# Batched matrix product: output copied out of PSUM in blocks of 32 partitions instead of 64, and one batch's blocks on VectorE

## The chip, the cores and the metric

The kernel runs on one core of a Trainium2 chip. The metric is the device time of one execution in microseconds (us). Before the change it is 136.78 us, the median of three runs (136.75 to 137.25).

The core's engines work side by side and wait for each other through semaphores: TensorE (PE in the profile; PEld is its weight load), VectorE (DVE), ScalarE (ACT), GpSimd (POOL) and SyncE (SP), which here only issues DMAs. Matrix products land in PSUM. VectorE and ScalarE copy them from there into SBUF, and DMAs carry them on to HBM. Each engine runs its instructions in the order in which they stand in the program.

## The reference

```python
batch, dim_i, dim_j, dim_k = 32, 256, 512, 384
# x: (batch, dim_i, dim_j) float32, y: (batch, dim_j, dim_k) float32

def reference(x, y):
    return np.einsum('bij,bjk->bik', x, y).astype(np.float32)
```

For each of 32 batches a 256x512 matrix is multiplied by a 512x384 matrix. The sum runs over j.

## The kernel before

**Stages.** The 32 batches are taken in N = 8 groups of Q = 4. Stage n handles batches 4n to 4n+3. Within a stage each batch has 32 partitions of its own in x, y and the weights: batch g has partitions 32g to 32g+31.

**Loads (lines 64 to 77).** `x_sb` has 128 partitions with 8 rows of 512 floats each (2 MB in all; each partition reads 16 KB in one run). `y_sb` has 128 partitions with 16 rows of 384 floats each (3 MB; 24 KB in one run). In the last stage y comes in four parts. SP issues all DMAs. There are two buffers each for x and y, so the load for stage n+2 waits until VectorE has cast stage n's data.

**x (lines 79 to 96), on VectorE.** x is cast to fp16 (`x_r`, line 83). Two neighbouring fp16 values are then taken as one 32-bit word and transposed in blocks of 32x32 words into `xt_sb`. `width(n)` chooses between two layouts. The 256 rows of a batch are spread over its 32 partitions, 8 rows each. Row r of a partition goes into half e (r modulo 2 in both layouts), and within the half it gets a column of the weights. With NARROW (64) the eight rows split as (b h e) with two values for each, and a transpose handles one e and one b: four transposes of 128x512 words a stage (line 96), with destination words two apart. With WIDE (32) they split as (h e) with four values of h, and a transpose handles one e: two transposes of 128x1024 words (line 90), with destination words next to each other. In both, source words are TW = 8 words apart. So the width sets which of a batch's 256 output rows lies in which partition of the result.

**y and the matmuls (lines 98 to 120).** y is cast to fp16 in four pieces on VectorE (line 107). After each piece come the matmuls for it: for both halves e, for the four t of the piece, for the four batches g, a matmul that contracts 32 partitions and adds into `ps_of[n][e][g]`, a PSUM tile of 128x384 floats. The four batches sit in four row tiles of the array. There are 128 matmuls a stage. The eight result tiles take all eight buffers of the PSUM pool (`bufs=2 * Q`), so a stage's matmuls into a tile wait until the stage before has been copied out of the same tile.

**Copying out (`collect`, lines 122 to 140).** With w = 64, `per` is 2: each of the eight result tiles is copied in two blocks of 64x384 into `o_sb`, 16 copies a stage. Two batches share the 128 partitions of an output part, 64 partitions each. All copies run on ScalarE, except in the last stage, where g = 1 and g = 3 go to VectorE.

**Stores (`store`, lines 142 to 153).** A partition of `o_sb` holds Q/`per` runs of output. With w = 64 those are two runs of 4 rows (6 KB), and each stage has two stores of 768 KB.

**Order (lines 155 to 166).** Every instruction is pinned to program order with `keep`. Two loads come first. Then for each n: cast and transpose x, cast y with the matmuls, copy out, load n+2, and store stage n−1. The last three stores (DEFER = 3) follow the loop. VectorE's order before is thus, for each stage: x cast, four transposes, four y casts; only in the last stage eight copies follow. SP's order is: x load n+2, y load n+2, stores of n−1.

Of the kernel before, what the change touches and what calls it, by code (L numbers as in the profile page):

```python
# [1 line left out]

# [5 lines left out]


MM_DT = mybir.dt.float16  # L10
F32 = mybir.dt.float32
P = 128


Q = 4
WIDE = 32
NARROW = 64

DEFER = 3


@with_exitstack
def kernel(
    ctx: ExitStack,
    tc: tile.TileContext,
    x: bass.AP,
    y: bass.AP,
    out: bass.AP,
):
    nc = tc.nc  # L30

    B, I, J = x.shape
    _, _, K = y.shape

    PQ = P // Q
    R = I // PQ
    T = J // PQ
    TW = T // 2
    NE = I // P
    N = B // Q  # L40

    x_pool = ctx.enter_context(tc.tile_pool(name="x_pool", bufs=2))
    y_pool = ctx.enter_context(tc.tile_pool(name="y_pool", bufs=2))
    xr_pool = ctx.enter_context(tc.tile_pool(name="xr_pool", bufs=1))
    xt_pool = ctx.enter_context(tc.tile_pool(name="xt_pool", bufs=2))
    yr_pool = ctx.enter_context(tc.tile_pool(name="yr_pool", bufs=2))
    o_pool = ctx.enter_context(tc.tile_pool(name="o_pool", bufs=DEFER + 2))
    psum_pool = ctx.enter_context(
        tc.tile_pool(name="psum", bufs=2 * Q, space=bass.MemoryType.PSUM)
    )  # L50

    keep = tc.keep_in_program_order

    x_of, y_of, xt_of, yr_of, ps_of, o_of = {}, {}, {}, {}, {}, {}

    def width(n):
        return NARROW

    def pieces(n):
        return 4

    def load(n):
        x_of[n] = x_pool.tile([P, R, J], F32, name="x_sb")
        keep(
            nc.sync.dma_start(  # L67
                out=x_of[n],
                in_=x[n * Q : (n + 1) * Q].rearrange("g (p r) j -> (g p) r j", r=R),
            )  # L70
        )
        y_of[n] = y_pool.tile([P, T, K], F32, name="y_sb")
        src = y[n * Q : (n + 1) * Q].rearrange("g (q t) k -> (g q) t k", t=T)
        parts = 4 if n == N - 1 else 1
        for a in range(parts):
            s = slice(a * T // parts, (a + 1) * T // parts)
            keep(nc.sync.dma_start(out=y_of[n][:, s], in_=src[:, s]))  # L77

    def transpose_x(n):


        x_r = xr_pool.tile([P, R, J], MM_DT, name="x_r")
        keep(nc.vector.tensor_copy(x_r, x_of.pop(n)))  # L83
        xt_of[n] = xt_pool.tile([P, NE, TW, P], F32, name="xt_sb")
        words = x_r.bitcast(F32)
        if width(n) == WIDE:
            src = words.rearrange("p (h e) (q t) -> p e t h q", e=NE, t=TW)
            dst = xt_of[n].rearrange("p e t (h s) -> p e t h s", s=PQ)
            for e in range(NE):
                keep(nc.vector.transpose(dst[:, e], src[:, e]))  # L90
        else:
            src = words.rearrange("p (b h e) (q t) -> p b e t h q", b=2, e=NE, t=TW)
            dst = xt_of[n].rearrange("p e t (h s b) -> p b e t h s", s=PQ, b=2)
            for e in range(NE):
                for b in range(2):
                    keep(nc.vector.transpose(dst[:, b, e], src[:, b, e]))  # L96

    def multiply(n):
        xt = xt_of.pop(n).bitcast(MM_DT).rearrange("p e t (m c) -> p e t m c", c=2)
        y_sb = y_of.pop(n)  # L100
        y_r = yr_pool.tile([P, T, K], MM_DT, name="y_r")
        ps_of[n] = [
            [psum_pool.tile([P, K], F32, name="o_ps") for _ in range(Q)] for _ in range(NE)
        ]
        step = T // pieces(n)
        for a in range(0, T, step):
            keep(nc.vector.tensor_copy(y_r[:, a : a + step], y_sb[:, a : a + step]))  # L107
            for e in range(NE):
                for t in range(a, a + step):
                    for g in range(Q):  # L110
                        s = slice(g * PQ, (g + 1) * PQ)
                        keep(
                            nc.tensor.matmul(  # L113
                                ps_of[n][e][g],
                                xt[s, e, t // 2, :, t % 2],
                                y_r[s, t],
                                start=(t == 0),
                                stop=(t == T - 1),
                            )
                        )  # L120

    def collect(n):
        w = width(n)
        per = P // w
        o_of[n] = o_pool.tile([P, R, K], F32, name="o_sb")
        o = o_of[n].rearrange("p (u f) k -> p u f k", u=Q // per)
        for u in range(Q // per):
            for e in range(NE):
                for v in range(per):
                    g = u * per + v  # L130
                    ps = ps_of[n][e][g]
                    on_vector = n == N - 1 and g % 2 == 1
                    for h in range(per):
                        src = ps[h * w : (h + 1) * w]
                        dst = o[v * w : (v + 1) * w, u, h * NE + e]
                        if on_vector:
                            keep(nc.vector.tensor_copy(dst, src))  # L137
                        else:
                            keep(nc.scalar.copy(dst, src))  # L139
        del ps_of[n]  # L140

    def store(n):
        w = width(n)
        per = P // w
        o = o_of.pop(n).rearrange("p (u f) k -> p u f k", u=Q // per)
        for u in range(Q // per):
            b = n * Q + u * per
            keep(
                nc.sync.dma_start(
                    out=out[b : b + per].rearrange("g (s f) k -> (g s) f k", s=w),  # L150
                    in_=o[:, u],
                )
            )

    for n in range(2):
        load(n)
    for n in range(N):
        transpose_x(n)
        multiply(n)
        collect(n)  # L160
        if n + 2 < N:
            load(n + 2)
        if n + 2 - DEFER >= 0 and n + 2 < N:
            store(n + 2 - DEFER)
    for n in range(N - DEFER, N):
        store(n)


# [1 line left out]
_INS = ['x', 'y']  # L170
_OUTS = [((32, 256, 384), 'float32')]


# [23 lines left out]
```

## Time and profile before

| What | Value |
|---|---|
| Median of three runs | 136.78 us |
| The profiled execution's own time | 137.25 us |
| Its span, first to last instruction | 135.5 us |
| TensorE (matmul) busy | 64.2 us, 47% |
| VectorE busy | 83.6 us, 62% |
| ScalarE busy | 58.0 us, 43% |
| Mean DMA rate over the span | 404 GB/s of 54.68 MB |
| Mean granted TensorE clock | 0.783 |

Some groups of instructions, as the page lists them:

| Line, engine | Instruction | Count | Mean ns |
|---|---|---|---|
| 83, VectorE | cast of x, 128x4096 | 8 | 2294 |
| 96, VectorE | transpose, 128x512 words | 32 | 1072 |
| 107, VectorE | cast of a piece of y, 128x1536 | 32 | 953 |
| 139, ScalarE | copy out of PSUM, 64x384 | 120 | 473 |
| 137, VectorE | copy out of PSUM, 64x384 | 8 | 556 |

How to read it: the span runs from the first to the last instruction of one execution. The chain of waits follows the work that ended last back to the start, at each step to what released it. A line of the timeline gives the start in us, the duration in us, the engine, the line of the code, the operation with output and input, its count, and in brackets how long the engine had been idle before and what released it. DMA rows cut the span into 40 equal slices, with a digit for the busy tenths of each.

The time at which each stage's x cast starts (line 83) is, in us: 8.80, 21.05, 34.26, 46.48, 63.46, 79.29, 95.63 and 111.82.

### The profile page before, as it was taken

The numbers are of one execution on the slowest core, as the hardware profiler recorded it, in microseconds if no ns is written. First come the engines' busy times: TensorE is split into PE (matmuls) and PEld (weight loads), VectorE is DVE, ScalarE is ACT, GpSimd is POOL, SyncE is SP. The second block draws the span as 40 slices with busy tenths as digits, with TensorE's granted clock in tenths as the row PEclk, the third lists the DMA queues.
The fourth block names the chain that finished last, engine by engine and source line by source line (L and its number), as shares of the span: only waits on it lengthen the run. The fifth ranks groups of instructions, "written<-read, shape, count | busy, mean of one in ns | idle before, by whom it ended". The sixth has DMA issues, their size and how long they took to land.

```text
span 135.5 us, 2381 instructions
## 1 busy us (share of the span) xinstructions
PE 64.2 (47%) x1024; PEld 33.7 (25%) x1024; DVE 83.6 (62%) x80; ACT 58.0 (43%) x121; POOL 0.2 (0%) x4
## 2 busy tenths in 40 slices
PE   0000099309934793579408940099302970089500
PEld 0000056104612361136104520045101540045200
DVE  0049777947897596822979059670796509990660
ACT  3000000894089408940794079500795039800640
POOL 0000000000000000000000000000000000000000
PEclk9999999975797579757975698556985698556985
DMA  4999999999999998999999999999999999999765
GB/s 111 426 431 457 414 445 450 389 428 474 392 435 421 435 399 339 442 441 450 398 399 453 423 457 385 415 431 457 418 385 417 441 409 419 415 421 426 302 279 210
DMA packets 5050, 54.68 MB, mean 404 GB/s; under 512 B 560, under 2 KB 560, under 8 KB 3120
## 3 DMA queue, kind: packets, MB, share of 16 engines
q1 hardware_dynamic: 5040, 54.53, 96.2%
q8 instruction: 8, 0.13, 0.4%
q14 instruction: 2, 0.02, 0.0%
HBM read 41.94 MB, written 12.58 MB: 402 GB/s over the span
## 4 chain that ended last, share of the span: by engine, by line
DMA 76%; DVE 13%; PE 5%; SPq 1%; issue 1%; DVEq 1%
DMA x_sb<-in_x_dram 76%; DVE x_r L83 7%; PE o_ps L113 5%; DVE xt_sb L96 3%; DVE o_sb L137 3%; DVE y_r L107 1%; DVEq L192 0%; SPq L77 0%; SPq L67 0%; DVEq L83 0%; DVEq L137 0%; DVEq L96 0%
## 5 line engine op out<-in xcount | busy, mean ns | idle before, releaser
L113 PE MATMUL o_ps<-y_r,xt_sb 32*128 32x384 f16 x1024 | 64.2, 415 | 62.9 <-DVE y_r L107 61.0
L139 ACT COPY o_sb<-o_ps 64x384 f32<-64x384 f32 x120 | 56.7, 473 | 71.6 <-PE o_ps L113 45.5
L113 PEld LDWEIGHTS <-xt_sb 32*128 32x128 f16 x1024 | 33.7, 116 | 93.0 <-DVE y_r L107 46.6
L83 DVE CAST x_r<-x_sb 128x4096 f16<-128x4096 f32 x8 | 18.4, 2294 | 33.3 <-DMA x_sb<-in_x_dram 33.3
L107 DVE CAST y_r<-y_sb 128x1536 f16<-128x1536 f32 x32 | 28.5, 953 | 8.6 <-DMA y_sb<-in_y_dram 8.6
L96 DVE STREAM_TRANSPOSE xt_sb<-x_r 128x512 f32<-128x512 f32 x32 | 32.4, 1072 | 0.7
L137 DVE COPY o_sb<-o_ps 64x384 f32<-64x384 f32 x8 | 4.4, 556 | 5.0 <-PE o_ps L113 4.8
L139 ACT ACT_TABLE_LOAD x1 | 1.3, 1283 | 0.7 <-PEq L181 0.7
L181 POOL MEMSET const-bfloat16-1.0<- 128x1 bf16 x1 | 0.1, 101 | 0.0
L181 POOL MEMSET const-uint8-127<- 128x1 uint8 x1 | 0.1, 101 | 0.0
L181 POOL MEMSET const-float32-0.0<- 128x1 f32 x1 | 0.1, 99 | 0.2 <-issue 0.2
L181 POOL MEMSET const-float32-1.0<- 128x1 f32 x1 | 0.1, 98 | 0.0
## 6 DMA issues: line engine op xcount, KB each, us to landing
y_sb<-in_y_dram SPq DMA_DIRECT2D x7, 3072.0 KB, 25.5
x_sb<-in_x_dram SPq DMA_DIRECT2D x8, 2048.0 KB, 24.9
out_dram<-o_sb SPq DMA_DIRECT2D x16, 768.0 KB, 20.6
y_sb<-in_y_dram SPq DMA_DIRECT2D x4, 768.0 KB, 24.1
```

Source lines behind the costliest of these rows:

```text
L83: keep(nc.vector.tensor_copy(x_r, x_of.pop(n)))
L96: keep(nc.vector.transpose(dst[:, b, e], src[:, b, e]))
L107: keep(nc.vector.tensor_copy(y_r[:, a : a + step], y_sb[:, a : a + step]))
L113: nc.tensor.matmul(ps_of[n][e][g], xt[s, e, t // 2, :, t % 2], y_r[s, t], start=(t == 0), stop=(t == T - 1),)
L137: keep(nc.vector.tensor_copy(dst, src))
L139: keep(nc.scalar.copy(dst, src))
L181: nc = _bacc.Bacc("TRN2", target_bir_lowering=False, num_devices=1)
```

## The change

Two lines differ. The stages before the last take the WIDE layout, and in those stages batch g = 3 of the four is copied out by VectorE.

```diff
@@ -56,7 +56,7 @@
     def width(n):
-        return NARROW
+        return NARROW if n == N - 1 else WIDE
@@ -129,7 +129,7 @@
                 for v in range(per):
                     g = u * per + v
                     ps = ps_of[n][e][g]
-                    on_vector = n == N - 1 and g % 2 == 1
+                    on_vector = g % 2 == 1 if n == N - 1 else g == Q - 1
                     for h in range(per):
```

What follows from `width`, in stages 0 to 6:

- Transposes on VectorE: two of 128x1024 words (line 90) in place of four of 128x512 (line 96).
- Copies out of PSUM: `per` is 4, so each result tile is copied in four blocks of 32x384, 32 copies a stage in place of 16. ScalarE has 24 of them (g = 0, 1, 2) and VectorE 8 (g = 3: four for e = 0, four for e = 1). Before, ScalarE had all 16 and VectorE none.
- VectorE's order: x cast, two transposes, four y casts, eight copies, and then the x cast of the next stage.
- Stores: each partition holds one run of 8 output rows (12 KB), and there is one store of 1.5 MB a stage in place of two of 768 KB.

The matmuls, the casts, the loads and their order are the same, and so is all of the last stage.

## The prediction

> **What bounds the kernel now.** I call the eight passes over four batches stages 0 to 7. I read the DMA rows of the page first, then the chain of waits, the table of windows from one x cast to the next, and last the timeline of VectorE and ScalarE.
>
> ```profile
> DMA  4999999999999998999999999999999999999765
> ...
> DMA x_sb<-in_x_dram 76%; DVE x_r L83 7%; PE o_ps L113 5%; DVE xt_sb L96 3%; DVE o_sb L137 3%; DVE y_r L107 1%; DVEq L192 0%; SPq L77 0%; SPq L67 0%; DVEq L83 0%; DVEq L137 0%; DVEq L96 0%
> ```
>
> The DMA engines are full from start to the last stage, and 76% of the chain is the wait for x. So memory traffic sets the pace; no engine does, until the tail.
>
> ```profile
> 63.46:79.29 15.83, 9.87 (x181) 5.23 (x173) 9.90 (x10) 8.04 (x17) 0.00 (x0) 0.78 1.01 429
> 79.29:95.63 16.34, 7.76 (x124) 4.02 (x124) 9.90 (x9) 7.17 (x16) 0.00 (x0) 0.69 0.99 414
> 95.63:111.82 16.19, 7.37 (x144) 3.71 (x132) 9.90 (x9) 8.78 (x19) 0.00 (x0) 0.79 1.00 419
> ```
>
> Columns: window, length, then busy us of PE, weight load, DVE, ACT, POOL, the granted clock, the DMA share and GB/s. A stage with its stores lasts some 16.2 us; VectorE is busy for 9.90 of it and ScalarE for about 8. Both look half free. The timeline says when they are free, and that decides this case:
>
> ```profile
> 70.65 3.57 DVE L107 CAST y_r<-y_sb 128x1536 f16<-128x1536 f32 x4 [0.76 <-DMA y_sb<-in_y_dram]
> 71.67 7.76 PE L113 MATMUL o_ps<-y_r,xt_sb 32*128 32x384 f16 x128 [5.96 <-DVE y_r L107]
> 78.81 7.83 ACT L139 COPY o_sb<-o_ps 64x384 f32<-64x384 f32 x16 [6.03 <-PE o_ps L113]
> 79.29 2.29 DVE L83 CAST x_r<-x_sb 128x4096 f16<-128x4096 f32 x1 [5.07 <-DMA x_sb<-in_x_dram]
> ```
>
> VectorE idles 5.07 us after its y casts, until x of the next stage lands at 79.29. TensorE has its first banks ready only at 78.81, 0.48 us before that. Only ScalarE copies out now, so VectorE waits for no matmul until the last stage:
>
> ```profile
> 111.82 2.29 DVE L83 CAST x_r<-x_sb 128x4096 f16<-128x4096 f32 x1 [5.09 <-DMA x_sb<-in_x_dram]
> 114.22 4.03 DVE L96 STREAM_TRANSPOSE xt_sb<-x_r 128x512 f32<-128x512 f32 x4
> 118.18 3.52 DVE L107 CAST y_r<-y_sb 128x1536 f16<-128x1536 f32 x4
> 119.15 7.91 PE L113 MATMUL o_ps<-y_r,xt_sb 32*128 32x384 f16 x128 [8.09 <-DVE y_r L107]
> 126.48 3.88 ACT L139 COPY o_sb<-o_ps 64x384 f32<-64x384 f32 x8 [8.18 <-issue]
> 126.54 4.56 DVE L137 COPY o_sb<-o_ps 64x384 f32<-64x384 f32 x8 [4.84 <-PE o_ps L113]
> ```
>
> There VectorE copies eight blocks, and cast, transpose, cast, matmuls and copies stand in one line: 111.82 to 131.10, or 19.28 us. The change gives stages 0 to 6 this shape.
>
> **The part that decides: eight copies on VectorE in stages 0 to 6.** VectorE runs in program order. Batch 3's copies (two halves of the rows, four blocks each) stand ahead of the next stage's x cast. Queued behind them are that cast, the transposes and the y casts; TensorE waits for those, and the copies wait for TensorE. No stage overlaps the next any more. The period, step by step from the last stage's lines:
> - x cast to first transpose: 114.22 − 111.82 = 2.40.
> - Transposes until the y cast: 118.18 − 114.22 = 3.96 (see below).
> - First y cast to first matmul: 119.15 − 118.18 = 0.97. The other three casts run beside the matmuls.
> - First matmul to first finished bank. In stages where TensorE didn't stall on ScalarE: 7.11, 7.43, 7.14, 7.54, 6.29 and 7.33 (stages 0, 1, 4 to 7), mean 7.14.
> - To the first VectorE copy: 126.54 − 126.48 = 0.06.
> - Eight copies: 4.56. The new ones have 32 partitions and 384 columns in place of 64 and 384; the second half of the rows is done about 0.6 us after the first (in stage 0 the matmuls end at 24.83, the first bank is ready at 24.20), so it is ready in time.
> - To the next cast: 0.02, an estimate from the semaphore events of 0.02 in the chain.
>
> Sum 19.11 us. Against 16.2 DMA no longer binds.
>
> **Copies of 32 partitions.** No row shows one. The casts cost 953 ns for 1536 columns and 2294 for 4096, so 0.52 ns a column and 148 fixed; a PSUM copy of 384 columns at 556 fits the same 148 with 1.06 a column. Time follows columns. If it followed partitions it would halve: 2.28 on VectorE. From above the slowest of the eight, 560, bounds it: 0.03 a stage more; no row costs more at fewer partitions. I take 556, the nearest row.
>
> **Transposes.** Two of 128x1024 replace four of 128x512; words, element type and the read stride of eight words are the same, and the write stride falls from two words to one. Four took 3.96 us, 1060 ns each at the median. By columns two take the same 3.96. The upper bound is the slowest single, 1121 ns for 512: 4 × 1.121 = 4.48. The lower is the x cast's 2294 / 4096 = 0.56 ns a column: 2 × 0.57 = 1.15. I take 3.96: same operation, same number of words.
>
> [...]
>
> **ScalarE.** Its copies go from 16 to 24 a stage. Sixteen took 7.83, so 0.4905 apart, and 24 take 23 × 0.4905 + 0.473 = 11.75 us after the first bank. All eight PSUM banks belong to one stage, so the next one's matmuls wait for them. They start 0.06 + 4.56 + 0.02 + 2.40 + 3.96 + 0.97 = 11.97 after that bank, and reach the second row half, whose banks come free last, four groups of 0.32 us later, at 13.25. So I cost the eight extra copies at nothing; VectorE's chain covers them by 1.5 us. Without that cover: the two stages of before in which TensorE stalled on ScalarE went on 0.05 after the copies and had a bank ready 5.71 and 5.75 later (45.62 to 51.33, 59.20 to 64.95). The period can't fall below 11.75 + 0.05 + 5.73 = 17.53.
>
> [...]
>
> **Stores, loads and SP.** Stages 0 to 6 store with one DMA of 1.5 MB in 12 KB runs, in place of two in 6 KB runs. A stage moves 2.10 + 3.15 + 1.57 = 6.82 MB; at the 419 GB/s of its window 16.3 us, inside 19.11. A faster rate gains nothing, and at the slowest row (414) it is 16.5, which loses nothing. SP's order stays: the x load of stage n+2 waits for the x cast of n, the y load for the y casts, and the store of n−1 behind them for ScalarE copies that ended 11.75 after their first bank, when those y casts end 14.6 after it. Every load is issued later, with VectorE, but about two periods (38 us) ahead of its use; with full queues x took 24.9 to land.
>
> **Sum.** Stage 0 runs as before up to its first bank at 24.20 (its y cast waits for y), and its copies end so that stage 1 casts x at 24.20 + 0.06 + 4.56 + 0.02 = 28.84, in place of 21.05. Six periods: 28.84 + 114.66 = 143.50 for the x cast of stage 7, in place of 111.82. Stage 7 is unchanged: 135.50 − 111.82 = 23.68. Span 167.2; with 137.25 − 135.50 = 1.75 around it, 168.9 by the profiled execution's own time. That is 0.47 above the median of the three runs, so **168.5 us**.
>
> **Rivals.**
> - Cheaper transposes, ScalarE sets the pace. For: the write is now contiguous. Against: the read stride stays. At the floor, first banks stand at 24.20 + 6 × 17.53 = 129.38 in stage 6, the last x cast 4.64 later at 134.02; 157.7 of span, 159.0 us. Lower transpose prices change nothing more.
> - Copies that cost half: period 16.83, last x cast 26.56 + 6 × 16.83 = 127.54, time 152.5. Only the partition count speaks for it.
> - TensorE stays at its slow pace. Idle between bursts grows from about 8 to 11.4 us. At 0.32 us for each of 32 groups the first bank comes near 9.9, 2.8 later: 6 × 2.8 more and stage 0 and 7 as well, some 190 us. Against: stage 0's burst, after 17 us of idle, took 7.74.
> - The other side: the copies fit into VectorE's idle. It is 5.07 us in each late stage and the copies are 4.56, so DMA would still bind: 136.8, or with 12 KB stores at up to the 428 GB/s of the load-only window in place of 414, 54.53 MB in 4.3 us less, down to 132.5. Against: at 78.81 only 0.48 of the 5.07 is left, and the delay adds up by stages. It decides only if first banks come 4.1 us sooner after the casts, at about 3.0 in place of 7.14.
> - The stores might not go out in longer runs. With DMA slack that changes nothing.
>
> **How the numbers follow.** Forecast 0.85 (its own range 165.5 to 172.5: first banks at 6.8 to 7.5 and part of the transposes' upper bound, whose 0.52 a stage is 3.1), cheaper transposes 0.06, cheaper copies 0.03, slow TensorE 0.03, other side 0.03. 158 to 173 takes in both of the transposes' bounds and leaves out about 0.1. Within 0.5%, 0.7 us, is about what this kernel's measurement can't tell from no change. Faster 0.015 and the same 0.015, both from the other side; slower 0.97.
>
> **What would show it.** Right: x casts 19.1 us apart, VectorE idle about 4.6 us before line 137 with TensorE as releaser in every stage, no wait for x after stage 1, DMA share near 0.8, transposes near 2.1 us each. Wrong: x still the releaser of the x cast, or line 139 the releaser of matmuls, or transposes near 1.1.

## The result, and the profile after

The changed kernel takes 165.57 us (median of four runs, 164.86 to 166.34). Its ratio to before is 1.210, with a 95% interval of 1.203 to 1.216. The forecast was 168.5 with a range of 158 to 173. The profiled execution took 165.37 us with a span of 163.5. Medians here and below are over all executions of a kernel; the ratios leave out three slow ones (over 1.5% above the fastest of their kernel) of later runs, 154.33 and 154.51 us with the halves in turn on the change (median of the other four 151.97) and 142.21 us with the stores split by partitions.

The DMA row and the chain of waits of the changed kernel's page:

```profile
DMA  5999999999998999999989899998997440009045
...
DVE o_sb L137 5%; PE o_ps L113 5%; DVE y_r L107 3%; DVE xt_sb L96 2%; DVE x_r L83 1%; DVEq L192 0%; DVEq L137 0%
```

The row has holes at the end now. The wait for x, 76% of the chain before, has left it: DMA no longer sets the pace. The chain that the page traces covers only the last stages, so I take the period from the timeline. It is the changed kernel's, with start, duration, engine, line and operation, and in brackets the idle time before and its releaser:

```profile
64.65 2.29 DVE L83 CAST x_r<-x_sb 128x4096 f16<-128x4096 f32 x1
66.98 3.90 DVE L90 STREAM_TRANSPOSE xt_sb<-x_r 128x1024 f32<-128x1024 f32 x2
70.80 3.52 DVE L107 CAST y_r<-y_sb 128x1536 f16<-128x1536 f32 x4
71.78 8.10 PE L113 MATMUL o_ps<-y_r,xt_sb 32*128 32x384 f16 x128 [11.19 <-DVE y_r L107]
79.25 11.62 ACT L139 COPY o_sb<-o_ps 32x384 f32<-32x384 f32 x24 [7.66 <-PE o_ps L113]
79.36 4.54 DVE L137 COPY o_sb<-o_ps 32x384 f32<-32x384 f32 x8 [5.03 <-PE o_ps L113]
83.93 2.29 DVE L83 CAST x_r<-x_sb 128x4096 f16<-128x4096 f32 x1
```

This is a middle stage with the shape that only the last stage had before. VectorE waits 5.03 us for matmuls, copies for 4.54, and casts the next x at once; x has long been there (its load was issued at 48.85, and x loads landed 13.2 us after their issue at the median), so no wait is named. TensorE waits 11.19 us for y casts that stand behind all of this. The x casts start at 8.38, 27.38, 46.52, 64.65, 83.93, 102.12, 121.50 and 139.74.

Two groups of the same kernel, with the shapes kept apart (busy us, mean ns of one, idle before):

```profile
L137 DVE COPY o_sb<-o_ps 32x384 f32<-32x384 f32 x56 | 31.1, 556 | 31.1 <-PE o_ps L113 21.3 <-issue 9.1
L90 DVE STREAM_TRANSPOSE xt_sb<-x_r 128x1024 f32<-128x1024 f32 x14 | 27.3, 1986 | 0.2
```

A copy of 32 partitions costs the 556 ns of one of 64. The transposes keep their price per word, but for a few per cent (1.94 ns against 2.07 before).

### The profile page after: what moved, and what is told of

Same layout as the page of the kernel before. It is cut to its first block, busy times and chain, and to the rows that moved or that the text cites. A ratio compares the mean times of both kernels' runs of the same rounds, so it can differ in the third digit from the quotient of the medians.

```text
span 163.5 us, 2460 instructions
## 1 busy us (share of the span) xinstructions
PE 59.8 (37%) x1024; PEld 31.2 (19%) x1024; DVE 112.9 (69%) x122; ACT 84.1 (51%) x177; POOL 0.2 (0%) x4
## 3 DMA queue, kind: packets, MB, share of 16 engines
q1 hardware_dynamic: 4032, 54.53, 81.9%
## 5 line engine op out<-in xcount | busy, mean ns | idle before, releaser
L139 ACT COPY o_sb<-o_ps 32x384 f32<-32x384 f32 (+1 forms) x176 | 82.8, 471 | 73.5 <-PE o_ps L113 48.9
L113 PE MATMUL o_ps<-y_r,xt_sb 32*128 32x384 f16 x1024 | 59.8, 405 | 95.2 <-DVE y_r L107 95.2
L137 DVE COPY o_sb<-o_ps 32x384 f32<-32x384 f32 (+1 forms) x64 | 35.6, 556 | 36.2 <-PE o_ps L113 26.3
L113 PEld LDWEIGHTS <-xt_sb 32*128 32x128 f16 x1024 | 31.2, 115 | 123.4 <-DVE y_r L107 81.2
L90 DVE STREAM_TRANSPOSE xt_sb<-x_r 128x1024 f32<-128x1024 f32 x14 | 27.3, 1986 | 0.2
L96 DVE STREAM_TRANSPOSE xt_sb<-x_r 128x512 f32<-128x512 f32 x4 | 4.0, 1058 | 0.0
## 6 DMA issues: line engine op xcount, KB each, us to landing
x_sb<-in_x_dram SPq DMA_DIRECT2D x8, 2048.0 KB, 13.2
```

What stands on the lines that cost most here:

```text
L113: nc.tensor.matmul(ps_of[n][e][g], xt[s, e, t // 2, :, t % 2], y_r[s, t], start=(t == 0), stop=(t == T - 1),)
```

## The experiments

Theory 1 is the forecast's: VectorE's copies stand between a stage's matmuls and the next stage's x cast, and so chain the stages together. Rival A is ScalarE's 24 copies, which hold the PSUM banks. Rival B is the layout: blocks of 32 partitions, wide transposes, one store. Ratios are against the kernel before, run on the same chip.

| Run | us | Ratio (95% interval) |
|---|---|---|
| before's layout, VectorE copies 8 a stage | 165.53 | 1.211 (1.206 to 1.215) |
| the change, all copies on ScalarE | 185.64 | 1.356 (1.351 to 1.361) |
| the change, VectorE's copies later | 154.79 | 1.133 (1.126 to 1.140) |
| before, wide transposes alone | 137.03 | 1.002 (0.999 to 1.004) |
| before, halves in turn | 136.75 | 1.001 (0.999 to 1.003) |
| the change, halves in turn | 152.51 | 1.113 (1.108 to 1.118) |
| wide in six stages, copies later, halves in turn | 135.54 | 0.991 (0.988 to 0.994) |
| the same, stores split by rows | 136.67 | 0.998 (0.996 to 1.001) |
| the same, stores split by partitions | 140.58 | 1.025 (1.022 to 1.029) |
| before, 3 KB runs | 136.80 | 0.999 (0.997 to 1.002) |

**VectorE's place alone.** The kernel before with one edit:

```diff
-                    on_vector = n == N - 1 and g % 2 == 1
+                    on_vector = g % 2 == 1
```

> The kernel of before (blocks of 64 partitions, four transposes, two stores a stage), with one edit: batches 1 and 3 are copied out by VectorE in every stage, not in the last alone. VectorE then has eight copies a stage as in the change, ScalarE has only eight, and blocks, layout and stores are those of before. Theory 1 (what costs the time is the place of VectorE's eight copies, between a stage's matmuls and the next stage's x cast): the period is the one forecast for the change, 18.7 to 19.1 us, so 165 to 169 us. Rival A (ScalarE's 24 copies hold the PSUM banks): with 8 copies that is gone, 137 to 140. Rival B (blocks of 32 partitions, or the wide layout with its transposes and stores): none of it is here, 137 to 140.

Measured 165.53, the time of the change (165.57), with none of its layout and with 8 copies a stage on ScalarE in place of 24. From that run's timeline and its waits (total us, times, longest):

```profile
42.76 4.54 DVE L137 COPY o_sb<-o_ps 64x384 f32<-64x384 f32 x8 [3.93 <-PE o_ps L113]
47.33 2.29 DVE L83 CAST x_r<-x_sb 128x4096 f16<-128x4096 f32 x1
...
DVE x_r L83 <- DMA x_sb<-in_x_dram: 8.5, 1, 8.5
```

The x cast follows the copies, and the only wait for x is that of stage 0. Rivals A and B fall: neither is needed for the whole loss.

**The wide transposes alone.**

```diff
-        if width(n) == WIDE:
+        if n < N - 1:
```

> The kernel of before with only the transposes of the change: in stages 0 to 6 two of 128x1024 words in place of four of 128x512. Copies, blocks and stores are those of before, so the output's rows stand in another order within each batch, and only the time is of use. Theory 1: 136.5 to 137.5, no difference, since transposes take 3.83 in place of 3.96 us and VectorE waits 5 us a stage for x. Rival B (the layout costs something by itself): above 139.

Measured 137.03, no difference that can be told. This excludes the wide transposes as a cause by themselves.

**The same work in another place.** The changed kernel with its VectorE copies put behind the next stage's x cast and transposes:

```diff
-                        if on_vector:
+                        if on_vector and n < N - 1:
+                            late.append((dst, src))
+                        elif on_vector:
                             keep(nc.vector.tensor_copy(dst, src))
...
         transpose_x(n)
+        for dst, src in late:
+            keep(nc.vector.tensor_copy(dst, src))
+        late.clear()
         multiply(n)
```

> The changed kernel with the same instructions on every engine; VectorE's eight copies of a stage stand later, behind the x cast and the transposes of the next stage and ahead of its y casts. Theory 1: VectorE no longer waits for the matmuls (they end about 1 us before the transposes do), its work is 14.3 us a stage, and ScalarE's 24 copies set the pace through PSUM: 11.62 + 0.05 + 5.73 = 17.4 us, first banks at 22.7 + 7 x 17.4 = 144.5 in stage 7, about 155 us. Rival B, or VectorE's amount of work as the cause: nothing of that changes, 164 to 167.

Measured 154.79: moving instructions, without taking any away, gives back 10.8 us. What then binds is in that run's timeline of VectorE, TensorE and ScalarE (line 164 is the late copy, 115 the matmul, 143 the ScalarE copy):

```profile
69.83 6.19 PE L115 MATMUL o_ps<-y_r,xt_sb 32*128 32x384 f16 x109 [1.46 <-ACT o_sb L143]
75.26 11.61 ACT L143 COPY o_sb<-o_ps 32x384 f32<-32x384 f32 x24 [5.47 <-PE o_ps L115]
75.41 4.54 DVE L164 COPY o_sb<-o_ps 32x384 f32<-32x384 f32 x8 [2.78 <-PE o_ps L115]
...
86.91 6.18 PE L115 MATMUL o_ps<-y_r,xt_sb 32*128 32x384 f16 x109 [1.46 <-ACT o_sb L143]
92.33 11.60 ACT L143 COPY o_sb<-o_ps 32x384 f32<-32x384 f32 x24 [5.47 <-PE o_ps L115]
```

TensorE waits for ScalarE's last banks, and ScalarE waits 5.47 us for TensorE: a loop of 92.33 − 75.26 = 17.07 us, close to the forecast's floor of 17.53. One thing was expected otherwise: VectorE still waits 2.78 us, because the stalled matmuls end later. So rival A is real, but it stands in second place, hidden in the change behind VectorE's 18.7.

**ScalarE alone.**

```diff
-                    on_vector = g % 2 == 1 if n == N - 1 else g == Q - 1
+                    on_vector = n == N - 1 and g % 2 == 1
```

> The changed kernel with all 32 copies of stages 0 to 6 on ScalarE; VectorE has none there, as before the change. Theory 1 with the PSUM floor of the prediction: VectorE's chain is gone, but ScalarE needs 31 x 0.485 + 0.47 = 15.5 us a stage, the next matmuls then end 0.05 + 5.73 later, so a period of 21.3 and first banks at 22.7 + 7 x 21.3 = 171.8, in the end about 183 us. If ScalarE's work can hide under DMA (15.5 is less than 16.2 a stage) and only VectorE's copies cost: 137 to 140.

Measured 185.64, expected about 183. ScalarE's first copies of a stage are 21.5 us apart in the mean of seven stages, expected 21.3. In that run's waits and its ScalarE timeline:

```profile
PE o_ps L113 <- ACT o_sb L139: 70.9, 53, 1.6
...
109.70 15.47 ACT L139 COPY o_sb<-o_ps 32x384 f32<-32x384 f32 x32 [5.49 <-PE o_ps L113]
132.16 15.46 ACT L139 COPY o_sb<-o_ps 32x384 f32<-32x384 f32 x32 [6.99 <-issue]
```

ScalarE's 15.47 us would fit inside a DMA stage of 16.2, but the wait for the banks puts it in line with the matmuls. Copies of half the height are twice as many and cost as much each (470 ns in the changed kernel, 473 before); in blocks of 64 partitions the same results take 16 copies and 7.83 us.

**Row halves in turn, on the change.** The matmuls of half 0 go with the y casts, then come all those of half 1:

```diff
-            for e in range(NE):
-                for t in range(a, a + step):
...
+            products(n, 0, a, step, xt, y_r)
+        products(n, 1, 0, T, xt, y_r)
```

> The changed kernel with the matmuls of the two row halves one after the other; VectorE's copies stay in their place ahead of the next x cast. Its four copies of half 0 then run beside the matmuls of half 1, and only four (2.28 us) follow them. Theory 1, with the terms measured after the change: 2.33 + 3.83 + 0.97 + 7.5 (all matmuls) + 0.06 + 2.28 + 0.03 = 17.0 a stage in place of 18.7, seven of them and a last stage shorter by up to 0.7: 151 to 155 us. If VectorE's amount of work or the 32-partition blocks set the time: unchanged, 164 to 167.

Measured 152.51. That run's timeline of VectorE in one stage (line 140 is the copy):

```profile
71.57 2.26 DVE L140 COPY o_sb<-o_ps 32x384 f32<-32x384 f32 x4 [2.39 <-PE o_ps L116]
74.17 2.26 DVE L140 COPY o_sb<-o_ps 32x384 f32<-32x384 f32 x4 [0.34 <-PE o_ps L116]
76.47 2.29 DVE L83 CAST x_r<-x_sb 128x4096 f16<-128x4096 f32 x1
```

Half of the copies now lies beside matmuls, which run from 66.64 to 74.04 in that stage. The x casts are 16.66 to 17.05 us apart, and no matmul waits for ScalarE. The chain's terms add up to the 17.0 expected when one of them is halved, which the rivals don't explain.

**The same on the kernel before.** Here `collect` also takes the halves in the outer loop.

```diff
-        for u in range(Q // per):
-            for e in range(NE):
+        for e in range(NE):
+            for u in range(Q // per):
```

> The kernel of before with the two row halves one after the other: the casts of y with the matmuls of half 0, then all matmuls of half 1, and the copies out in that order. The first banks are ready after half of the matmuls, about 5.1 us after the first (16 groups at 0.32), in place of 7.3. In stages 0 to 6 DMA hides it. In the last stage half 0's four VectorE copies (2.28) run beside the matmuls of half 1, and only 2.28 us of copies follow the end at 7.8: 0.06 + 10.1 in place of 7.33 + 0.06 + 4.56 = 11.95 from the first matmul, 1.7 less. Theory 1: 134.7 to 135.6. If the tail is set by the last stores and not by the copies: 136.5 to 137.

Measured 136.75, ratio 1.001: a miss for theory 1. The last VectorE copies of that run, SyncE's issues of the last two stores (a merged line runs from the start of the first to the end of the last), and, last, the same two stores in the kernel before:

```profile
127.57 2.28 DVE L140 COPY o_sb<-o_ps 64x384 f32<-64x384 f32 x4 [0.27 <-PE o_ps L116]
128.76 1.49 SPq L152 DMA_DIRECT2D out_dram<-o_sb  x2
...
128.87 2.63 SPq L149 DMA_DIRECT2D out_dram<-o_sb  x2
```

The engines do save what was expected: from the last x cast to the end of the copies it takes 17.42 us in place of 19.28. That cast starts 0.61 later in this execution (112.43), so the copies end at 129.85 in place of 131.10. Yet the span is 135.6 in place of 135.5. Each of the last stage's two stores needs both row halves. So the first is issued at 128.76, hardly before the 128.87 of the kernel before, and only the second comes earlier, right behind it. The earlier stores are nearly through by then (DMA share 0.37 from 128 to 129 us); from 130 to 133 us the share is 0.99 to 1.05, and SyncE waits 4.3 us for the last store in place of 2.9. What was saved on the copies is lost in DMA, which has two stores to move at the end. The chain of waits, which ends with VectorE's last copy, doesn't show this.

**A version with DMA as its bound.** Wide blocks in stages 0 to 5, late copies, halves in turn; stages 6 and 7 as in the run just told.

```diff
-        return NARROW if n == N - 1 else WIDE
+        return NARROW if n >= N - 2 else WIDE
...
-                    on_vector = g % 2 == 1 if n == N - 1 else g == Q - 1
+                    on_vector = g % 2 == 1 if n == N - 1 else g == Q - 1 and w == WIDE
```

> Wide blocks, one 1.5 MB store and VectorE's copies of one batch in stages 0 to 5 alone; those copies stand behind the next stage's transposes, and the row halves follow one another. Stages 6 and 7 are those of the run of the kernel of before with row halves, which is its control. VectorE has 14.3 us a stage and ScalarE 11.6, both less than the 16.2 of DMA, and banks come free in time, so DMA binds again. What it tells apart: whether 12 KB stores are worth anything where DMA binds. Without worth: as the control, 134.5 to 136. With the rate of the load-only window (428 in place of 414 GB/s): up to 4 us less than the control, from 131.

Measured 135.54, ratio 0.991 (0.988 to 0.994): a little faster than before, and than its control at 136.75. It has the change's copies on both engines in six stages, and none of its loss. In its timeline VectorE waits for x again:

```profile
94.95 2.29 DVE L83 CAST x_r<-x_sb 128x4096 f16<-128x4096 f32 x1 [1.40 <-DMA x_sb<-in_x_dram]
110.83 2.29 DVE L83 CAST x_r<-x_sb 128x4096 f16<-128x4096 f32 x1 [1.34 <-DMA x_sb<-in_x_dram]
```

**What the long stores are worth.** Three runs. First the kernel just told, each 1.5 MB store split by rows of a partition:

```diff
+            rows = R * per // Q
+            step = 4
+            for a in range(0, rows, step):
+                f = slice(a, a + step)
...
-                    out=out[b : b + per].rearrange("g (s f) k -> (g s) f k", s=w),
-                    in_=o[:, u],
+                        out=out[b : b + per].rearrange("g (s f) k -> (g s) f k", s=w)[:, f],
+                        in_=o[:, u, f],
```

> The run with wide blocks in stages 0 to 5, late copies and row halves (135.54 us, 0.9% under before), with each 1.5 MB store of 12 KB runs split in two of 768 KB with 6 KB runs, as before the change; nothing else differs. If the longer runs are what made that kernel faster: its gain is gone, 136.5 to 137. If it is the new order on VectorE, which casts x as soon as it is there and moves the y loads later in the queue: 135.3 to 135.9.

Measured 136.67: the gain is gone. Next the kernel before, its stores split in the same way with steps of 2 rows:

> The kernel of before, in which DMA binds, with each store of 768 KB in 6 KB runs split in two of 384 KB with 3 KB runs. If the length of a run has a price where DMA binds, and 6 to 12 KB is worth 1.2 us, 6 to 3 KB costs about 2.4 more, twice the runs added: 138 to 140. If runs of these lengths cost nothing: 136.3 to 137.2.

Measured 136.80, no price at all. Last the 135.54 us kernel with the stores split by partitions:

```diff
+            parts = 2 if w == WIDE else 1
+            for a in range(parts):
+                q = slice(a * P // parts, (a + 1) * P // parts)
...
-                    out=out[b : b + per].rearrange("g (s f) k -> (g s) f k", s=w),
-                    in_=o[:, u],
+                        out=out[b : b + per].rearrange("g (s f) k -> (g s) f k", s=w)[q],
+                        in_=o[q, u],
```

> The same 135.54 us run once more with its 1.5 MB stores split in two, now by partitions: two of 64 partitions each, and the runs stay at 12 KB. The count of stores is that of the split by rows (136.67 us), the length of a run that of the unsplit one. If the length of the runs brings the 1.1 us: 135.3 to 135.9. If the count of stores costs it (each of the eight DMA semaphores comes round sooner, and SP waits for it ahead of later issues): 136.4 to 137.

Measured 140.58, outside both branches. Windows of 30 us (window, length, busy us of each engine, clock, DMA share, GB/s), first in the 135.54 us kernel:

```profile
30.00:60.00 30.00, 15.02 (x256) 7.58 (x256) 29.59 (x33) 22.11 (x48) 0.00 (x0) 0.73 1.00 423
60.00:90.00 30.00, 13.65 (x256) 7.26 (x256) 28.77 (x32) 24.47 (x53) 0.00 (x0) 0.73 1.01 430
```

and with the stores of 64 partitions:

```profile
30.00:60.00 30.00, 14.55 (x256) 7.42 (x256) 29.59 (x33) 22.15 (x48) 0.00 (x0) 0.73 1.00 409
60.00:90.00 30.00, 14.87 (x256) 7.63 (x256) 27.85 (x30) 23.08 (x50) 0.00 (x0) 0.73 1.00 414
```

The DMA engines are as full (shares of 1.00 and 1.00, against 1.00 and 1.01) and move less, 409 and 414 in place of 423 and 430 GB/s. Eight semaphores for DMAs stand in the trace of before, where its 35 DMA issues take them in turn. The two splits have the same count of stores, and SyncE's store issues wait about as long for earlier DMAs, 16.0 us in all by rows and 15.7 by partitions (none with unsplit stores). So the count can't explain the 3.9 us between 136.67 and 140.58: in this kernel a store of 64 partitions has a price of its own. For that reason this run can't tell the length of a run from the count of stores. That one store of 1.5 MB is worth about 1.1 us in that schedule is shown; whether by its longer runs or by being one is open.

## Why the prediction was right

**The decisive step held.** A period made of cast, transposes, cast, matmuls and copies, read off the last stage of before, is what stages 0 to 6 became. It was shown by its place alone (165.53 us with nothing else of the change) and by moving it away.

**The terms.** The time was 2.9 us under the forecast, at the lower edge of its own range (165.5 to 172.5). In the profiled execution:

| Term | Forecast | Measured |
|---|---|---|
| x cast to first transpose | 2.40 | 2.33 |
| transposes until the y cast | 3.96 | 3.83 |
| first y cast to first matmul | 0.97 | 0.97 |
| first matmul to first bank, mean of stages 1 to 6 | 7.14 | 6.92 |
| to the first VectorE copy | 0.06 | 0.10 |
| eight copies and handover | 4.58 | 4.57 |
| period | 19.11 | 18.72 |

Six periods account for 6 × 0.39 = 2.3 us of the 3.7 by which the span (163.5) is under its forecast (167.2). Stage 0 ended 1.46 earlier (27.38 in place of 28.84): x landed 0.42 sooner, and its first bank came 6.04 us after the first matmul, in place of 7.11. Stage 7 took 23.76, forecast 23.68. So the mis-sized terms are the first bank's and, by a few per cent, the transposes'.

**The first bank's term** was taken as a mean of six bursts of before, from 6.29 to 7.54. In the changed kernel it alternates: 7.35, 6.32, 7.47, 6.39, 7.56, 6.42. That their mean, 6.92, lies so near 7.14 is partly luck: nothing in the forecast fixed how long after its first matmul a new burst would see the clock rise. Three windows of 0.5 us each in stages 1 and 2 (the last three columns: granted clock, DMA share, GB/s):

```profile
38.90:39.40 0.50, 0.50 (x12) 0.28 (x8) 0.00 (x0) 0.00 (x0) 0.00 (x0) 0.50 0.89 377
39.40:39.90 0.50, 0.50 (x16) 0.23 (x12) 0.00 (x0) 0.00 (x0) 0.00 (x0) 0.60 0.93 393
39.90:40.40 0.50, 0.50 (x20) 0.31 (x16) 0.00 (x0) 0.00 (x0) 0.00 (x0) 1.00 1.04 442
...
56.10:56.60 0.50, 0.50 (x12) 0.25 (x8) 0.10 (x1) 0.00 (x0) 0.00 (x0) 0.50 1.01 434
56.60:57.10 0.50, 0.50 (x16) 0.27 (x12) 0.00 (x0) 0.00 (x0) 0.00 (x0) 0.73 0.96 410
57.10:57.60 0.50, 0.50 (x20) 0.31 (x16) 0.00 (x0) 0.00 (x0) 0.00 (x0) 1.00 1.01 434
```

The clock rises from 0.5 to 1.0 some 5.1 us after the first matmul (34.50) in the one stage and 3.2 after it (53.65) in the other.

**Transposes.** 1986 ns for 1024 words, or 1.94 a word against 2.07 before. The wide form brought 6%, not half; the run with the wide transposes alone shows that this is worth nothing where DMA binds (137.03, ratio 1.002). Whether the unit write stride brought it is not shown: there are also half as many instructions, and 2 × 1060 − 1986 = 134 ns is near the 148 ns fixed that the forecast found in the casts and left out here. The transposes near 1.1 us, which the forecast names as a sign against it, are shown by no run: the wide ones took 1.96 to 2.01.

**ScalarE at nothing** held: 24 copies took 11.62 us (11.75 forecast), and no matmul of the changed kernel waits for ScalarE. The floor behind that cover was 17.07 in place of 17.53 when it was laid open.

**Stores and loads at nothing** held too: the only wait for x is stage 0's, and the DMA queue's share fell from 96.2% to 81.9%.

**Rivals.** The other side, copies that fit into VectorE's 5 us of idle, fell as argued: the idle came before the banks were ready. With the copies late, the halves in turn and the wide blocks in six stages only, the idle could be used, and the time did come to 135.54. Copies at half price and a slow TensorE did not occur.

**One reading was too simple.** The forecast said that no engine sets the pace until the tail. The tail isn't the engines' alone: the halves in turn on the kernel before ended the copies 1.25 us earlier and gained nothing, as DMA still had the last two stores to move.

## What to carry to other kernels

An engine that is half idle can't take work for nothing: ask when its idle time lies, and what stands behind the new work in its queue. Here 4.5 us of copies fitted into 5 us of idle by their size, and cost 21% because they waited for the stage's matmuls ahead of the next stage's first cast; put behind that cast and the transposes, the same copies gave 10.8 us back, and what then bound was ScalarE's 24 copies. And count the blocks in which PSUM is emptied: a copy of 32 partitions took the 556 ns of one of 64, so halving the height doubled the work.

## What the runs showed of the hardware

The clock's rises in the changed kernel stand at 39.6, 56.8, 77.2, 94.2, 114.7, 131.8 and 152.4 us, by the points at which the weight loads begin to run without gaps: 17.0 to 17.2 and 20.4 to 20.6 apart, by turns. Where the rise came 3.2 us after the first matmul of a stage, the first bank took 6.32 to 6.42 us; where it came 5.1 to 5.4 after it, 7.35 to 7.56. Two neighbouring distances between rises add up to 37.4 to 37.7 us, and two neighbouring periods of the x casts to 37.3 to 37.6.

I had not expected that loops settle near the shorter of these distances. With the copies late, first banks come 17.07 to 17.12 us apart in all seven stages; with the halves in turn on the change, x casts are 16.66, 16.87, 16.96, 17.01, 17.04 and 17.05 apart, moving towards the same value. My guess is that the clock's rises hold the loops there. No run shows that, nor what sets the times of the rises.

The other finding is the price of a store of 64 partitions: with two such stores in place of one of 128 the same kernel took 140.58 in place of 135.54 us, and 3.9 us more than with two of 128 partitions and half the run (136.67).
